# A hybrid decoder layer on one core: where the retention states of the sample tokens are weighted by their queries

## The chip, the cores and the metric

The kernel runs on one core of a Trainium2 chip. Its time is the device time of one execution in microseconds (us): 2566.66 us as the median of three runs (2566.41 to 2567.9). The engines are named as the profile names them: PE (TensorE's matmuls) and PEld (its weight loads), DVE (VectorE), ACT (ScalarE), POOL (GpSimd), and SP (SyncE), whose queue issues the DMAs.

## The reference, cut to what matters

One layer of a decoder is computed for 256 prompt tokens with 16 meta tokens ahead of them, and for 8 sample tokens, one each from eight other requests. The model is 2048 wide. A half-step SwiGLU block, a token mixer and a second half-step SwiGLU block follow one another. The mixer multiplies the input by ten matrices of 2048 x 2048, runs two recurrences on the projections, retention (8 heads of 256 x 256 state) and HGRN2 (16 heads of 128 x 128 state), gates their outputs with sigmoids and multiplies the sum by an output matrix.

For a sample token a retention head does this (one state S of 256 x 256 for each of the 8 requests and each head):

```
S_new = gamma * S + outer(k, v)
o     = q @ S_new          # written here for one token; 256 numbers
```

So a sample's output is its new state, each of its 256 rows multiplied by one number of the query, summed over the rows. The states are outputs too. All inputs and outputs are fp32.

## The kernel before, in words

**Weights.** Every large matrix is read from memory once, in fp32, in *units* of 512 KB: eight blocks of 128 x 128. `load` (L185 to L189) brings a unit into a buffer `raw` by a DMA on SP's queue, ACT rounds it to a first part `whi` (L188), and DVE subtracts to get the rest, `wlo` (L189). Each of the three tiles has three buffers. A DMA for a later unit can start when the `wlo` three units earlier has been computed, and ACT can write a `whi` when PE has finished with the unit three places earlier. PE multiplies each block three times (L218: `xh` by `whi`, `xl` by `whi`, `xh` by `wlo`), so a unit is 24 matmuls of 264 or 280 columns.

**The mixer.** The retention heads and the HGRN2 heads are worked on in eight *steps of heads* u = 0 to 7, one retention head and two HGRN2 heads each. For each u, `project(qkv_groups(u))` computes six pairs of column groups (the pair named `f` first, then `q_h`, `i_h`, and the three of retention), and then `project(gate_groups(u - 1))` computes the gates of the heads before: four groups, in the order g_r with a_r, g_h with a_h, and the two again for the second half. The names of the PSUM tiles begin with `pj_`. One group is 16 inner steps (k = 0 to 15) of two blocks each: four weight units. After every inner step the function `pump` is called. It advances the two generators `mix_hg` and `mix_ret`, which hold everything else of the mixer; `yield n` in one of them lets n inner steps pass. So a `yield` sets between which weight matmuls the small matmuls of the recurrences stand on PE. PE's order is the order in which the program is written. The order on the other engines is set by a scheduler that goes by priorities; the casts of the weights have a higher priority.

**Sample outputs in retention** (end of `mix_ret`). For each u the eight new states lie in four tiles `smr` of 128 x (4 x 256), called `sms[2 * e + c]` in the code: e is the half of the samples, c the half of the 256 rows. They are computed by ACT (L1192) and DVE (L1198) and stored by SP (L1202, `out_srs`). Then 16 fp32 matmuls (L1211) multiply each 128 x 256 piece by a column of the query. The stationary operand is a slice of `qdr`, 128 x 32, zero but for one column; `alone` (L733) has placed the queries so. Four matmuls, for four samples, run in four quarters of PE's columns. The two halves e and c add up in PSUM (`pqr`). The matmuls of HGRN2's samples (L1039, `pq`) stand right ahead of them. After seven more steps the outputs are transposed and added (`po`, `por`), and normalised from there (`pv`, `pvr`); the gate of the g_r group then uses them (`on_r`).

Of the kernel before, what the change touches and what calls it, by code (L numbers as in the profile page):

```python
# [13 lines left out]
AF = mybir.ActivationFunctionType  # L14
ALU = mybir.AluOpType
# [8 lines left out]
NMETA, SEQ, NS = 16, 256, 8  # L24
# [104 lines left out]
def trunk(ctx: ExitStack, tc: tile.TileContext, A, O):  # L129
    nc = tc.nc  # L130
# [108 lines left out]
    def mul(out, a, b):  # L239
        nc.vector.tensor_tensor(out=out, in0=a, in1=b, op=ALU.mult)  # L240

    def bias(b):
        return {} if b is None else {"bias": b}

    def mul_biased(out, o, b, x):
        if b is None:
            mul(out, x, o)
        else:
            nc.vector.scalar_tensor_tensor(out=out, in0=o, scalar=b, in1=x, op0=ALU.add, op1=ALU.mult)

    def add(out, a, b):
        nc.vector.tensor_tensor(out=out, in0=a, in1=b, op=ALU.add)
# [294 lines left out]
    with tc.tile_pool(name="yp", bufs=1) as yp:  # L547
# [7 lines left out]
        with tc.tile_pool(name="mp", bufs=1) as mp:  # L555
# [7 lines left out]
            def tmp(name, shape=(P, T), bufs=1, dt=F32, tag=None):  # L563
                if name in rows:
                    rows[name] = rows[name][1:] + rows[name][:1]
                    return rp.tile(list(shape), dt, tag=rows[name][-1], name=name)
                return mp.tile(list(shape), dt, tag=tag or name, name=name, bufs=bufs)
# [16 lines left out]
            st = {}  # L584
# [5 lines left out]
            qdr = tmp("qdr", (P, 4, ALONE))  # L590
            nc.gpsimd.memset(qdh, 0.0)
            nc.gpsimd.memset(qdr, 0.0)
            qdh_at = [qdh.rearrange("p a c -> p (a c)")[:, 256 * h :] for h in range(2)]
            qdr_at = [qdr.rearrange("p a c -> p (a c)")[:, 2 * ALONE * c :] for c in range(2)]
            vsm = tmp("vsm", (P, P))
            vt2 = tmp("vt2", (P, 2, P))
# [20 lines left out]
            def pump(_=None):  # L617

                for th in list(threads):
                    th[1] -= 1  # L620
                    if th[1] <= 0:
                        th[1] = next(th[0], None)
                        if th[1] is None:
                            threads.remove(th)

            def start(gen, wait):
                threads.append([gen, wait])
# [20 lines left out]
            def evacuate(n, c0, c1, o0, o1, b0, b1):  # L648
                if n == "f":
                    f = tmp("f", (P, 2, T))  # L650
                    k = tmp("k", (P, 2, T))
                    for j, (c, o, b) in enumerate(((c0, o0, b0), (c1, o1, b1))):
                        nc.scalar.activation(f[:, j, :], o, AF.Sigmoid, **bias(b))
                        nc.scalar.activation(f[:, j, :], f[:, j, :], AF.Identity, scale=olb[:, c : c + 1], bias=lb[:, c : c + 1])
                    nc.scalar.activation(k, f, AF.Identity, scale=-1.0, bias=1.0)
                    st["f"], st["k"] = f, k
                elif n == "q_h":
                    q = tmp("q", (P, 2, TL))
                    for j, (o, b) in enumerate(((o0, b0), (o1, b1))):
                        nc.scalar.activation(q[:, j, :], o, AF.Sigmoid, **bias(b))  # L660
                        mul_biased(q[:, j, :], o, b, q[:, j, :])
                    st["q"] = q
                elif n == "i_h":
                    v = st.pop("i_h", None)
                    if v is None:
                        v = tmp("v", (P, 2, T))
                        nc.scalar.copy(v[:, 0, :], o0)
                        nc.scalar.copy(v[:, 1, :], o1)

                    start(mix_hg(c0 // 2, st["f"], st["k"], st["q"], v), {0: 20, 2: 46}.get(c0, 4))  # L670
                elif n in ("q_r", "k_r"):
                    sc, w, x0 = (1.0, TL, NMETA) if n == "q_r" else (KSC, T, 0)
                    r = tmp(n, (P, 2, w))
                    for j, (a, b, op) in enumerate(((cos, sin, ALU.subtract), (sin, cos, ALU.add))):
                        t = tmp("rot", (P, w), bufs=2)
                        for to, o, s, x in ((r[:, j, :], o0, b0, a), (t, o1, b1, b)):
                            nc.vector.scalar_tensor_tensor(
                                out=to, in0=o, scalar=sc if s is None else s, in1=x[:, x0:],
                                op0=ALU.mult if s is None else ALU.add, op1=ALU.mult)
                        nc.vector.tensor_tensor(out=r[:, j, :], in0=r[:, j, :], in1=t, op=op)  # L680
                    st[n] = r
                elif n == "v_r":
                    v = tmp("v", (P, 2, T))
                    nc.scalar.copy(v[:, 0, :], o0)
                    nc.scalar.copy(v[:, 1, :], o1)
                    start(mix_ret(c0 // 2, st["q_r"], st["k_r"], v), 24 if c0 == 2 else 3)
                elif n in ("g_r", "g_h"):
                    sg = tmp("gs", (P, TL), bufs=2)
                    t = tmp("gt", (P, TL), bufs=2)
                    nc.scalar.activation(sg, o0, AF.Sigmoid)  # L690
                    mul(t, sg, o0)
                    sa = tmp("gs", (P, TL), bufs=2)
                    nc.scalar.activation(sa, o1, AF.Sigmoid)
                    mul(t, t, sa)
                    u, e = divmod(c0, 2)
                    while u not in (done_r if n == "g_r" else done_h):
                        pump()
                    if n == "g_r":
                        y = tmp("y", (P, TL))
                        mul(y, t, on_r[u][:, e, :])  # L700
                        st["y"] = y
                    else:
                        y = st["y"]
                        nc.vector.scalar_tensor_tensor(
                            out=t, in0=t, scalar=ngt[:, c0 : c0 + 1], in1=on_h[u][:, e, :], op0=ALU.mult, op1=ALU.mult)

                        ys[c0] = y if c0 < EARLY else yp.tile([P, TL], F32, tag=f"y{c0}", name=f"y{c0}")
                        add(ys[c0], y, t)
                        if c0 < EARLY:
                            split(yh[c0], yl[c0], y)  # L710
# [22 lines left out]
            def alone(qd, q):  # L733
                nc.vector.tensor_copy(
                    qd[:, :, : 128 : 32].rearrange("p (c e) j -> p c e j", e=2),
                    q[:, :, SEQ:].rearrange("p c (e j) -> p c e j", e=2))
# [9 lines left out]
            def mix_hg(u, f, k, q, v):  # L746

                calm = 2
# [14 lines left out]
                sms, vbs = [], []  # L763
# [254 lines left out]
                for h in range(2):  # L1018
# [7 lines left out]
                    for b in range(2):  # L1026
                        nc.vector.scalar_tensor_tensor(
                            out=S[:, b + 1, :], in0=S[:, b, :], scalar=Tt[:, h, b : b + 1],
                            in1=pst[:, (b + 1) * P : (b + 2) * P], op0=ALU.mult, op1=ALU.add)
                    nc.sync.dma_start(O["sgp"][2 * u + h], S[:, 2, :])  # L1030
                if u == 1:
                    yield 2
                    samples(1)
                yield (8, 11, 45)[min(u, 2)]
                pq = mx_bank("pq")
                for h in range(2):
                    for b in range(NS):
                        j = 32 * (b % 4)
                        nc.tensor.matmul(  # L1039
                            pq[j : j + 32, :P], qdh_at[h][:, 32 * b : 32 * b + 32], sms[h][:, b, :],  # L1040
                            start=h == 0 and b < 4, stop=h == 1 and b >= 4, tile_position=(0, j))
# [26 lines left out]
                calm = calm if u else 0  # L1068
# [16 lines left out]
            def mix_ret(u, q, k, v):  # L1085
# [3 lines left out]
                calm = 2  # L1089
                sms = []  # L1090
# [13 lines left out]
                for c in range(2):  # L1104
# [22 lines left out]
                    for x, g, his, i, lo in todo:  # L1127
                        for hi in his:
                            nc.scalar.activation(hi, x, AF.Copy, scale=g)
                        nc.vector.scalar_tensor_tensor(  # L1130
                            out=lo, in0=x, scalar=g, in1=his[i].bitcast(F32), op0=ALU.mult, op1=ALU.subtract)
                    yield 2
                alone(qdr, q)
                vts = [vt[:, 0], vt[:, 1], vs2]
                vrow = rows_out(vt2.rearrange("p c f -> p (c f)")[16:24, :], 256, "vr")

# [25 lines left out]
                for c in range(2):  # L1162
# [9 lines left out]
                    if c == 0:  # L1172
                        gams = [tmp("gam", (P, 1))]
                        nc.gpsimd.tensor_scalar(
                            out=gams[0], in0=so[:, 0:1], scalar1=GAMMA[u], scalar2=GAMMA[u], op0=ALU.min, op1=ALU.max)
# [13 lines left out]
                for e in range(2):  # L1189
# [3 lines left out]
                    for i in (2 * e, 2 * e + 1):  # L1193
                        for c in range(2):
                            for b in (2 * i, 2 * i + 1):
# [3 lines left out]
                                    out=x, in0=vbs[i][:, b - 2 * i, :], scalar=kk, in1=x, op0=ALU.mult, op1=ALU.add)  # L1199
# [1 line left out]
                    for c in range(2):  # L1201
                        nc.sync.dma_start(O["srs"][u, c, :, 4 * e : 4 * e + 4, :], ss[c])  # L1202
                    yield 1 if e else 10 if u == 0 else 6
                yield (11 if u == 0 else 15) + 2 * calm
                pq = mx_bank("pqr")
                scores(pq[:, 256:], 2)
                for e in range(2):
                    for c in range(2):
                        for j in range(4):
                            b = 4 * e + j  # L1210
                            nc.tensor.matmul(  # L1211
                                pq[32 * j : 32 * j + 32, :256], qdr_at[c][:, 32 * b : 32 * b + 32],
                                sms[2 * e + c][:, j, :], start=e + c == 0, stop=e + c == 2, tile_position=(0, 32 * j))
                mul(scr2[:NB2], pq[:NB2, 256 : 256 + NMETA], dt[:NB2, c2:])
                upper_upper_lower(sc2, scr2[:NB2])
                os = tmp("osr", (P, 256))
# [160 lines left out]
```

## Time and profile before

| What | Value |
|---|---|
| median of three runs | 2566.66 us |
| the profiled execution's span | 2563.9 us |
| PE, share of the span and instructions | 2553.4 us, 100%, 23424 |
| DVE | 1702.8 us, 66%, 2827 |
| ACT | 1392.2 us, 54%, 2186 |
| POOL | 57.0 us, 2%, 152 |
| DMA, bytes and mean rate | 536.26 MB, 209 GB/s |

The execution that was profiled spans 2563.9 us between its first and its last instruction; the median of the timed runs is 2.8 us longer, which is what lies around the span. The mixer's steps of heads fill about 825 to 1760 us of the span; the SwiGLU blocks lie ahead of and behind it. A row of the timeline gives start, duration, engine, line, operation and tiles, and, in brackets, the idle time of that engine just before and what ended it. A number with an x behind a row says how many instructions it stands for. PE's matmuls are pipelined: the distance between two starts says more than the duration of one.

### The profile page before, as it was taken

To read this page: it belongs to the slowest core of one execution; us is meant where nothing else is said; L and a number is where in the kernel's file an instruction comes from. 1 tells how busy PE (TensorE), PEld (TensorE's weight loads), DVE (VectorE), ACT (ScalarE), POOL (GpSimd) and SP (SyncE) were. 2 spreads that over 40 slices of the span, in tenths; PEclk is the share of its full clock that TensorE was granted. 3 is DMA by queue.
4 is the path that set the end of the run, shared out by engine and by line. 5 is a ranking of instruction groups with operands and counts; after the bars stand their busy time and mean duration, and the time that the engine had idled before them with its cause. 6 is when DMAs were issued, how large, how long until landed. Compare 5 with 4: busy or idle time off the path is not lost.

```text
span 2563.9 us, 56275 instructions
## 1 busy us (share of the span) xinstructions
PE 2553.4 (100%) x23424; PEld 2534.4 (99%) x23424; DVE 1702.8 (66%) x2827; ACT 1392.2 (54%) x2186; POOL 57.0 (2%) x152
## 2 busy tenths in 40 slices
PE   9999999999999999999999999999999999999999
PEld 9999999999999999999999999999999999999998
DVE  6444544475569878777777777777885555556555
ACT  5444444444456767767676666675564444444443
POOL 0000000000000000000000000000000000000000
PEclk9999999999999999999999999999999999999999
DMA  7555555555555876767676767675556565565554
GB/s 244 183 187 183 187 182 184 186 182 186 184 201 180 287 265 232 264 214 260 212 264 215 259 223 255 224 239 188 196 190 197 194 197 195 194 196 195 195 195 149
DMA packets 156897, 536.26 MB, mean 209 GB/s; under 512 B 17952, under 2 KB 25952, under 8 KB 156640
## 3 DMA queue, kind: packets, MB, share of 16 engines
q1 hardware_dynamic: 156352, 532.37, 62.0%
q8 instruction: 183, 3.00, 0.5%
q14 instruction: 74, 0.61, 0.1%
q10 hardware_dynamic: 288, 0.29, 0.0%
HBM read 501.99 MB, written 30.61 MB: 208 GB/s over the span
## 4 chain that ended last, share of the span: by engine, by line
PE 96%; DVE 2%; ACT 0%; issue 0%; DMA 0%; SPq 0%; ACTq 0%; DVEq 0%
PE up L218 36%; PE dn L218 19%; PE pj_i_h L218 3%; PE pj_g_r L218 3%; PE pj_q_h L218 3%; PE pj_g_h L218 3%; PE pj_a_r L218 3%; PE pj_a_h L218 3%; PE pj_f L218 3%; PE pj_q_r L218 3%; PE pj_k_r L218 3%; PE wo L218 3%; PE pj_v_r L218 3%; DVE wlo L189 1%; PE pqr L1211 1%; PE psr L1168 0%
## 5 line engine op out<-in xcount | busy, mean ns | idle before, releaser
L189 DVE TENSOR_TENSOR wlo<-raw,whi 128x1024 fp32r<-128x1024 f32 (+1 forms) x869 | 1062.2, 1223 | 740.7 <-ACT whi L188 737.3
L188 ACT CAST whi<-raw 128x1024 fp32r<-128x1024 f32 (+1 forms) x870 | 905.7, 1042 | 909.2 <-PE up L218 411.0
L218 PE MATMUL up<-xh,whi 128*128 128x280 f32 (+1 forms) x2624 | 725.6, 280 | 0.6 <-ACT whi L188 0.6
L218 PE MATMUL up<-xh,wlo 128*128 128x280 f32 (+1 forms) x2624 | 725.8, 280 | 0.4 <-DVE wlo L189 0.3
L218 PE MATMUL up<-xl,whi 128*128 128x280 f32 (+1 forms) x2624 | 725.4, 279 | 0.0
L218 PEld LDWEIGHTS up<-xh,wlo 128*128 128x128 f32 x2624 | 492.6, 189 | 1.0 <-DVE wlo L189 1.0
L218 PEld LDWEIGHTS up<-xh,whi 128*128 128x128 f32 x2624 | 492.6, 189 | 0.8 <-ACT whi L188 0.8
L218 PEld LDWEIGHTS up<-xl,whi 128*128 128x128 f32 x2624 | 492.6, 189 | 0.0
L218 PE MATMUL dn<-hh,whi 128*128 128x280 f32 (+1 forms) x1376 | 384.7, 280 | 0.0
L218 PE MATMUL dn<-hh,wlo 128*128 128x280 f32 (+1 forms) x1376 | 384.3, 279 | 0.0
L218 PE MATMUL dn<-hl,whi 128*128 128x280 f32 (+1 forms) x1376 | 384.3, 279 | 0.0
L218 PEld LDWEIGHTS dn<-hh,whi 128*128 128x128 f32 x1376 | 260.1, 189 | 0.1
L218 PEld LDWEIGHTS dn<-hl,whi 128*128 128x128 f32 x1376 | 260.1, 189 | 0.1
L218 PEld LDWEIGHTS dn<-hh,wlo 128*128 128x128 f32 x1376 | 260.1, 189 | 0.0
L218 PE MATMUL pj_k_r<-xh,whi 128*128 128x280 f32 x256 | 74.2, 290 | 0.0
L218 PE MATMUL pj_g_r<-xh,whi 128*128 128x264 f32 x256 | 74.0, 289 | 0.0
L218 PE MATMUL pj_v_r<-xh,whi 128*128 128x280 f32 x256 | 73.8, 288 | 0.0
L218 PE MATMUL pj_v_r<-xh,wlo 128*128 128x280 f32 x256 | 72.4, 283 | 0.3 <-DVE wlo L189 0.3
L218 PE MATMUL pj_g_h<-xh,whi 128*128 128x264 f32 x256 | 72.7, 284 | 0.0
L218 PE MATMUL pj_k_r<-xh,wlo 128*128 128x280 f32 x256 | 72.4, 283 | 0.0
L218 PE MATMUL pj_v_r<-xl,whi 128*128 128x280 f32 x256 | 72.3, 283 | 0.0
L218 PE MATMUL pj_k_r<-xl,whi 128*128 128x280 f32 x256 | 72.3, 283 | 0.0
(421 smaller groups left out, 5263.4 us busy)
## 6 DMA issues: line engine op xcount, KB each, us to landing
raw<-in_w_up SPq DMA_DIRECT2D x343, 512.0 KB, 4.1
raw<-in_w_in SPq DMA_DIRECT2D x320, 512.0 KB, 4.3
raw<-in_w_dn SPq DMA_DIRECT2D x172, 512.0 KB, 3.5
smr<-in_sr SPq DMA_DIRECT2D x32, 512.0 KB, 5.0
out_srs<-smr SPq DMA_DIRECT2D x32, 512.0 KB, 6.7
raw<-in_w_out SPq DMA_DIRECT2D x32, 512.0 KB, 3.9
vbr<-vrd SPq DMA_DIRECT2D x32, 256.0 KB, 4.1
smh<-in_sg SPq DMA_DIRECT2D x16, 512.0 KB, 5.2
```

The lines of the kernel that those rows point to most:

```text
L188: nc.scalar.copy(hi[:, j:jn, :], raw[:, j:jn, :])
L189: nc.vector.tensor_tensor(out=lo[:, j0:j1, :], in0=raw[:, j0:j1, :], in1=hi[:, j0:j1, :].bitcast(F32), op=ALU.subtract)
L218: nc.tensor.matmul(o, w, t, start=start, stop=stop)
L1211: nc.tensor.matmul(pq[32 * j : 32 * j + 32, :256], qdr_at[c][:, 32 * b : 32 * b + 32], sms[2 * e + c][:, j, :], start=e + c == 0, stop=e + ...
```

## The change

For u = 2 to 7 (the *third unit* of heads onward) the two halves c of a sample's state are combined ahead of the matmul. GpSimd (for e = 0, new line L1223) or ScalarE (e = 1, L1221) multiplies the 128 x 256 piece of c = 0 by its queries, one number for each partition, and VectorE (L1224) multiplies the piece of c = 1 by its queries and adds. That is 4 operations on GpSimd, 4 on ScalarE and 8 on VectorE for each u. Then 8 matmuls instead of 16 (L1233) sum over the partitions; their stationary operand `one` is zero but for a column of ones.

The queries are copied by GpSimd to `late_q` (L1215). A copy ahead of it (L1214) reads the newest sigmoid of a gate, `seen`, and so holds GpSimd's work until that tile is there. VectorE's copy in `alone` is left out from u = 2 on. For u = 2 GpSimd also writes zeros and ones once.

The waits in steps change too: 45 becomes 67 in `mix_hg`, and 15 + 4 becomes 25 + 16 in `mix_ret`, with the new operations between the two. So both sets of sample matmuls, and everything behind them in the generators, come 22 inner steps later in PE's order. u = 0 and 1 stay as they are.

```diff
             qdr = tmp("qdr", (P, 4, ALONE))
...
+            one = qdr[:, 0, :64].rearrange("p (e m) -> p e m", e=2)
+            late_q = qdr[:, 1, : 2 * NS].rearrange("p (c b) -> p c b", c=2)
...
                     nc.scalar.activation(sa, o1, AF.Sigmoid)
+                    st["seen"] = sa
                     mul(t, t, sa)
...
-                yield (8, 11, 45)[min(u, 2)]
+                yield (8, 11, 67)[min(u, 2)]
                 pq = mx_bank("pq")
...
-                alone(qdr, q)
+                if u < 2:
+                    alone(qdr, q)
...
-                yield (11 if u == 0 else 15) + 2 * calm
+                yield (11 if u == 0 else 15) + 2 * calm if u < 2 else 25
+                if u == 2:
+                    nc.gpsimd.memset(qdr[:, 0, :64], 0.0)
+                    for e in range(2):
+                        nc.gpsimd.memset(one[:, e, e : e + 1], 1.0)
+                if u > 1:
+                    nc.gpsimd.tensor_copy(late_q[:, 0, :1], st["seen"][:, :1])
+                    nc.gpsimd.tensor_copy(late_q, q[:, :, SEQ:])
+                    for e in range(2):
+                        s0, s1 = sms[2 * e : 2 * e + 2]
+                        for b in range(4):
+                            g = [late_q[:, c, 4 * e + b : 4 * e + b + 1] for c in range(2)]
+                            if e:
+                                nc.scalar.activation(s0[:, b, :], s0[:, b, :], AF.Copy, scale=g[0])
+                            else:
+                                nc.gpsimd.tensor_scalar(out=s0[:, b, :], in0=s0[:, b, :], scalar1=g[0], scalar2=None, op0=ALU.mult)
+                            nc.vector.scalar_tensor_tensor(
+                                out=s0[:, b, :], in0=s1[:, b, :], scalar=g[1], in1=s0[:, b, :], op0=ALU.mult, op1=ALU.add)
+                    yield 16
                 pq = mx_bank("pqr")
                 scores(pq[:, 256:], 2)
                 for e in range(2):
-                    for c in range(2):
+                    for c in range(2 if u < 2 else 1):
                         for j in range(4):
                             b = 4 * e + j
                             nc.tensor.matmul(
-                                pq[32 * j : 32 * j + 32, :256], qdr_at[c][:, 32 * b : 32 * b + 32],
-                                sms[2 * e + c][:, j, :], start=e + c == 0, stop=e + c == 2, tile_position=(0, 32 * j))
+                                pq[32 * j : 32 * j + 32, :256], qdr_at[c][:, 32 * b : 32 * b + 32] if u < 2 else one[:, e, :],
+                                sms[2 * e + c][:, j, :], start=e + c == 0, stop=e + c == 2 if u < 2 else e == 1, tile_position=(0, 32 * j))
```

The order of the engines' instructions before and after is shown for u = 3, on three engines. PE first, at the sample matmuls. Before, they stand inside a g_r/a_r group, after its inner step 10:

```order
L218 MATMUL pj_a_r_15214<-xh_10_9275,wlo_15277 128x264
L1039 MATMUL pq<-smh,qdh 32x128 x16
L1141 MATMUL pqr<-q_r,k_r 16x16 x2
L1211 MATMUL pqr<-smr,qdr 32x256 x16
L218 MATMUL pj_g_r_15213<-xh_11_9279,whi_15276 128x264
```

After the change they stand behind the first inner step of the next u's `f` group, 22 steps later, and the last set has half as many:

```order
L218 MATMUL pj_f_15506<-xh_0_9235,wlo_15509 128x280
L1042 MATMUL pq<-smh,qdh 32x128 x16
L1145 MATMUL pqr<-q_r,k_r 16x16 x2
L1233 MATMUL pqr<-smr,qdr 32x256 x8
L218 MATMUL pj_f_15505<-xh_1_9239,whi_15508 128x280
```

So two weight groups less one step run on PE without the sample matmuls between their steps, and the first step of `f` now has them behind it.

On DVE the place is the stretch from g_r's inner step 8 to the next `f` group. The names `gt` and `y` are gate products, `scr`, `sc`, `cen` and `osr` follow the sample matmuls. Before:

```order
L189 TENSOR_TENSOR wlo_15396<-raw_15394,whi_15395 128x8x128
L240 TENSOR_TENSOR scr_8637<-pqr,dtab 16x16
L255 TENSOR_TENSOR sc_8642<-scr_8637,sc_8642 16x16
L1081 TENSOR_REDUCE cen<-osr 128x1
L1082 TENSOR_SCALAR cen<-cen 128x1
L1083 TENSOR_TENSOR osr<-osr,cen 128x256
L189 TENSOR_TENSOR wlo_15465<-raw_15463,whi_15464 128x8x128
L240 TENSOR_TENSOR gt<-gs,pj_g_r_15213 128x264
L189 TENSOR_TENSOR wlo_15495<-raw_15493,whi_15494 128x8x128
L240 TENSOR_TENSOR gt<-gt,gs 128x264
L742 COPY on_h<-po 128x2x8
```

After:

```order
L189 TENSOR_TENSOR wlo_15407<-raw_15405,whi_15406 128x8x128
L240 TENSOR_TENSOR gt<-gs,pj_g_r_15224 128x264
L189 TENSOR_TENSOR wlo_15437<-raw_15435,whi_15436 128x8x128
L240 TENSOR_TENSOR gt<-gt,gs 128x264
L1224 SCALAR_TENSOR_TENSOR smr<-smr,qdr 128x256
L240 TENSOR_TENSOR y<-gt,on_r 128x264
L1224 SCALAR_TENSOR_TENSOR smr<-smr,qdr 128x256 x3
L189 TENSOR_TENSOR wlo_15467<-raw_15465,whi_15466 128x8x128
L1224 SCALAR_TENSOR_TENSOR smr<-smr,qdr 128x256 x4
L189 TENSOR_TENSOR wlo_15509<-raw_15507,whi_15508 128x8x128
```

The small operations behind the sample matmuls have left this stretch; four of the new operations stand between two casts of weights, and four more between the next two.

On ACT, in the same stretch after the change (`gs` are the sigmoids of the gates; the fourth row makes the tile that `seen` names):

```order
L188 CAST whi_15406<-raw_15405 128x8x128
L692 ACTIVATE gs<-pj_g_r_15224 128x264
L188 CAST whi_15436<-raw_15435 128x8x128
L695 ACTIVATE gs<-pj_a_r_15225 128x264
L1221 ACTIVATE smr<-smr,qdr 128x256 x4
L188 CAST whi_15466<-raw_15465 128x8x128
```

ACT's four multiplications stand between two casts. GpSimd's whole order there, after the change, is this:

```order
L1192 COPY sro<-k_r 128x8
L1214 COPY qdr<-gs 128x1
L1215 COPY qdr<-q_r 128x16
L1223 TENSOR_SCALAR smr<-smr,qdr 128x256 x4
L913 COPY meta<-K 128x2x16
```

Before the change, the second, third and fourth of these rows are not there.

## The prediction

> **What bounds the kernel now.** I read the page's busy times first, then the chain of waits, then single stretches of the timeline.
>
> ```profile
> PE 2553.4 (100%) x23424; PEld 2534.4 (99%) x23424; DVE 1702.8 (66%) x2827; ACT 1392.2 (54%) x2186; POOL 57.0 (2%) x152
> PE 96%; DVE 2%; ACT 0%; issue 0%; DMA 0%; SPq 0%; ACTq 0%; DVEq 0%
> ```
>
> PE is busy all the time and 96% of the chain is its own work. So the only certain gain is matmul time taken away, and any new wait of PE is added to the time. The matmuls at issue, for u = 3:
>
> ```profile
> 1190.44 0.28 PE L218 MATMUL pj_a_r<-xh,wlo 128*128 128x264 f32 x1
> 1190.65 1.08 PE L1039 MATMUL pq<-smh,qdh 128*32 128x128 f32 x32
> 1191.65 1.89 PE L1211 MATMUL pqr<-smr,qdr 128*32 128x256 f32 x29
> 1193.47 0.38 PE L218 MATMUL pj_g_r<-xh,whi 128*128 128x264 f32 x1
> ```
>
> The weight matmuls before and after the sample matmuls start 3.03 us apart (1193.47 - 1190.44); their usual pitch is 10.80 / 96 = 0.1125 us by the next rows, which each count one whole group of columns by 96 matmuls:
>
> ```profile
> 1097.31 10.80 PE pj_q_h L218 x96
> 1108.11 11.44 PE pj_i_h L218 x96
> ```
>
> A weight unit is 24 matmuls: 2.70 us (264 columns) or 2.86 us (280 columns). PE never stalls there, but by how little?
>
> ```profile
> 1188.64 0.19 PEld L218 LDWEIGHTS pj_g_r<-xh,wlo 128*128 128x128 f32 x1
> 1202.49 0.19 PEld L218 LDWEIGHTS pj_g_h<-xh,wlo 128*128 128x128 f32 x1
> 1187.26 1.22 DVE L189 TENSOR_TENSOR wlo<-raw,whi 128x1024 fp32r<-128x1024 f32 x1
> 1196.02 1.23 DVE L189 TENSOR_TENSOR wlo<-raw,whi 128x1024 fp32r<-128x1024 f32 x1 [0.21 <-ACT whi L188]
> 1198.47 1.23 DVE L189 TENSOR_TENSOR wlo<-raw,whi 128x1024 fp32r<-128x1024 f32 x1 [0.81 <-ACT whi L188]
> ```
>
> The first row is PE's first use of `wlo` of the unit that holds inner steps 8 to 11 of g_r; call that unit A. Its `wlo` was ready at 1187.26 + 1.22 = 1188.48, 0.16 us before. Three units later (A+3, second row) the `wlo` of 1196.02 was ready 5.24 us early. What made that slack is not a faster supply. It is PE's pauses: from 1188.64 to 1202.49 are 13.85 us for three units of 2.70 us, so 5.75 us went to small matmuls (`pq`, `pqr`, `po`, `por`). The supply itself is at its limit, as the windows show (us, then busy time of PE, PEld, DVE, ACT, POOL, the granted clock, the DMA share, GB/s):
>
> ```profile
> 1168.00:1188.00 20.00, 20.00 (x181) 20.00 (x180) 16.95 (x33) 13.52 (x20) 1.40 (x3) 1.00 0.82 275
> 1188.00:1202.00 14.00, 14.00 (x165) 12.85 (x164) 9.97 (x22) 7.48 (x15) 0.00 (x0) 1.00 0.96 332
> 1211.00:1224.00 13.00, 13.00 (x112) 13.00 (x111) 11.10 (x21) 10.74 (x16) 0.00 (x0) 1.00 0.50 157
> 1194.94 1.05 ACT L188 CAST whi<-raw 128x1024 fp32r<-128x1024 f32 x1 [0.23 <-DMA raw<-in_w_in]
> 1197.39 1.04 ACT L188 CAST whi<-raw 128x1024 fp32r<-128x1024 f32 x1 [0.19 <-DMA raw<-in_w_in]
> 1191.35 0.33 SPq L185 DMA_DIRECT2D raw<-in_w_in  x1
> ```
>
> The DMA engines are 0.96 busy from 1188 to 1202, and the casts of A+3 and A+4 (1194.94, 1197.39) end waits for DMAs; the `raw` of the latter was issued at 1191.35, 6 us earlier. So the supply has no reserve just where the change takes PE's pauses out.
>
> **The change part by part. What it removes:** 8 of 16 matmuls for each u, which run four at a time, so 8 rounds become 4. A round takes (1.89 - 0.38) / 7 = 0.216 us (0.38 is one matmul, next row), so 0.86 us for each u and 6 x 0.86 = 5.2 us in all. That is 0.2% of the time and the most that can be won.
>
> ```profile
> L1211 PE MATMUL pqr<-smr,qdr x256: 379/379/403, 859.8 to 1698.6; 128*32 128x256 f32 x128
> ```
>
> **What it moves.** The sample matmuls and what follows them leave A to A+5 and stand 22 steps later. PE then wants the weights early: counted from 1188.64, A+3 at +8.10 (1196.74), A+5 at +13.50 (1202.14), A+6, the first unit of `f`, at +16.20. Against the ends of `wlo` above: A+3 was ready at 1197.25, so **0.5 us of stall**. A+4's cast ended 1199.70 (1198.47 + 1.23) and was needed at 1199.44 + 0.5, so it holds. Neither comes earlier by the change, since both hang on DMAs issued before anything that has moved. The DVE work that leaves (`scr` to `osr`) was behind those waits, too.
>
> **What it adds** comes behind A+4's cast, ahead of A+5's on both engines. Prices:
>
> ```profile
> 1182.61 2.06 DVE L1198 SCALAR_TENSOR_TENSOR smr<-vbr,sro,smr 128x256 f32<-128x256 f32 x5
> 1199.61 0.43 DVE L240 TENSOR_TENSOR gt<-gt,gs 128x264 f32<-128x264 f32 x1
> 1198.35 0.38 ACT L693 ACTIVATE gs<-pj_a_r 128x264 f32<-128x264 f32 x1
> L998 ACT ACTIVATE smh<-smh,meta 128x128 f32<-128x128 f32 x128 | 41.1, 391 | 0.4
> L1192 ACT ACTIVATE smr<-smr,gam 128x1024 f32<-128x1024 f32 x16 | 17.6, 1142 | 9.2 <-POOL gam L1174 9.2
> 1148.36 0.23 POOL L1103 COPY tails<-k_r 128x48 f32<-128x48 f32 x1 [4.01 <-DVE k_r L680]
> 1172.35 0.19 POOL L1188 COPY sro<-k_r 128x8 f32<-128x8 f32 x1
> 1170.10 1.21 DVE L189 TENSOR_TENSOR wlo<-raw,whi 128x1024 fp32r<-128x1024 f32 x1
> 1170.18 1.17 POOL L1174 TENSOR_SCALAR gam<-sro 128x1 f32<-128x1 f32 x1 [9.92 <-ACT sro L1170]
> ```
>
> - DVE, multiply and add: 2.06 / 5 = 0.41 us each, eight for each u (3.3 us).
> - ACT, 128 x 256: between 0.38 (264 columns) and 391 + 128 x (1142 - 391) / 896 = 498 ns. I take 0.44.
> - GpSimd, 128 x 256: no row has it. From 8 and 48 columns follow 0.001 us a column, so 0.23 + 208 x 0.001 = 0.44; I take 0.42 and keep 0.6 as the upper end. The dearest row is `gam`, 1.17 us for a single column, but it ends with the `wlo` that runs beside it (1171.35 and 1171.31), so I read it as 0.2 us behind a wait. It also tells that GpSimd doesn't proceed beside a DVE operation of two SBUF tiles. The new operations on DVE are of that kind, so I take the two engines as taking turns.
>
> The Trainium skill says so outright ("SBUF — State Buffer", "Who interferes with whom"): GpSimd and an operation of VectorE with two inputs in SBUF hold a shared port exclusively, and the later one blocks. The `gam` row agrees (1.17 against 0.19 us). That the new operation on VectorE takes the port is shown by no run here; by that rule the sum is the one below, without it the lower bound.
>
> For u = 3: `seen` is ready at 1198.73 (1198.35 + 0.38), GpSimd gets through after A+4's `wlo` at 1199.70, two short copies of 0.2 us and their hand-overs make 1200.2. Four turns of 0.42 + 0.41 and `y` (0.43, like `gt`) between them end at 1203.95, A+5's `wlo` at 1205.2. ACT meanwhile goes 1200.2 + 4 x 0.44 + 1.05 = 1203.0, so it isn't last. PE needs A+5 at 1202.14 + 0.5 = 1202.64: **2.5 us of stall**. Then four more additions and a cast on DVE, 1205.2 + 1.65 + 1.23 = 1208.1, against 1202.64 + 2.5 + 2.70 = 1207.84: **0.3 us**. In `f` the sample matmuls give PE its pause back, about 2.2 us, and the stall ends. Sum for u = 3: 3.3 us.
>
> The other five u have a better start. u = 4, by the same three places:
>
> ```profile
> 1314.98 0.19 PEld L218 LDWEIGHTS pj_g_r<-xh,wlo 128*128 128x128 f32 x1
> 1320.88 1.05 ACT L188 CAST whi<-raw 128x1024 fp32r<-128x1024 f32 x1
> 1324.50 1.23 DVE L189 TENSOR_TENSOR wlo<-raw,whi 128x1024 fp32r<-128x1024 f32 x1 [0.50 <-ACT whi L188]
> ```
>
> A+4's `wlo` ends 10.75 us after A's use (11.06 in u = 3), and the cast of A+3 stood behind ACT's copies of the sample outputs, which move away, so perhaps 10.5. The chain of 5.5 us from there (1199.70 to 1205.2) ends at 16.0 against 13.5 plus 0.1: 2.4, and 0.1 to 0.3 around it; I take 2.5. **Sum: 3.3 + 5 x 2.5 = 15.8 us of new stalls, less 5.2 us of matmuls: +10.6 us.** The span goes from 2563.9 to 2574.5, and with the 2.76 us by which the median of 2566.66 lies above the span, to **2577 us**.
>
> **At no cost:** GpSimd's writes of ones (u = 2, once), two copies and the missing `alone` are off PE's path; without their 0.5 us the chain would begin at 1199.7, so they are in it. The next u's two loads of states, which SP issued behind `pqr`, now wait for the additions and stand behind two weight loads on the queue; nobody needs them before the next u, and they delay no weight before A+5. In `f` the cover is thin (DVE 11.10 and ACT 10.74 of 13 us, third window), but PE's own pauses move there with the work. At u = 7 no `f` follows, and the gate forces `pvr` two steps early; I bound that at two steps, 1.35 us, once, and take 0.
>
> **Bounds.** Low: GpSimd works beside DVE. Then u = 3 ends A+5's `wlo` by ACT's path, 1203.0 + 1.23 = 1204.25, 1.6 us of stall and 2.4 in all; the others, from 10.5, 1.35 each: 9.2 - 5.2 = +4.0, 2570.7 us. High: 0.6 for a GpSimd operation, four turns longer by 0.7 us, six times: +4.3, 2581.5 us; and a chain that starts 0.25 later each (no gain from ACT's copies) 2583.
>
> **The rivals.**
>
> *A: no stall, 2561.5 us (not slower).* The loads leave the queue's worst stretch, each `raw` lands sooner, and the chain fits. It needs A+5's `wlo` 2.5 us earlier. The next row gives the wait from issue to landing; the two loads of states, 1 MB, make about 3 us of the queue at 332 GB/s.
>
> ```profile
> raw<-in_w_in SPq DMA_DIRECT2D x8, 512.0 KB, 5.8
> ```
>
> It decides where `raw` comes in 4.3 us and both engines work side by side (1.5 + 1.0 us). Against it: the `raw` of A+4 was issued at 1191.35, ahead of those loads, which follow `pqr`. Gain 5.2 us.
>
> *B: a mild stall, 2567 to 2571.8 us.* The lower bound above, or part of the DMA gain of A: some 0.9 to 1.7 us a u.
>
> *C: GpSimd's operations cost what the one long row says,* 1.17 us each, with DVE's hidden beneath. u = 3: 1200.2 + 4 x 1.17 + 0.41 + 1.23 = 1206.5, so 3.9 instead of 2.5; six times 1.3 to 1.4 more: +8, 2585 us. Against it: the row has a wait in it. For it: no row of this size exists.
>
> *D: the change doesn't reach PE,* because PE now waits for the additions at `pqr`. They are done by 1207 (four behind A+5's cast), `pqr` stands at about 1209; 0 to 1 us each. It would raise the forecast by up to 5, inside C's range.
>
> **How the numbers follow.** The likeliest case, stalls of 2 to 3 us a u, 2571.8 to 2583 us: 0.48. C and D above 2583: 0.20. B: 0.22. A: 0.10. A measurement of this kernel tells 0.2% from no change, 5.1 us. So: faster (below 2561.5) only in the better half of A and a little beyond, 0.08, since the whole gain is just 0.2%; the same (2561.5 to 2571.8) in B and the rest of A, 0.21; slower 0.71. Predicted 2577 us, range 2564 to 2586 us; the likeliest case alone has 2571.8 to 2583.
>
> **What would show it.** `pqr` with 8 matmuls in about 1.05 us; idle time of PE before weight loads of A+3 and A+5, put down to `wlo` (DVE), some 2 to 3 us for each u; four turns of GpSimd and DVE of 0.83 us between two casts. Wrong if the additions overlap GpSimd's multiplications and end by 1202.7, if `raw` of A+4 lands more than a microsecond earlier, or if PE stalls in the `f` group instead.

## The result and the profile after

| | before | after |
|---|---|---|
| median | 2566.6 us | 2587.91 us (2585.29 to 2589.8) |
| ratio | | 1.0082, 95% interval 1.0068 to 1.0097 |
| span of the profiled execution | 2563.9 us | 2584.9 us |

The change makes the kernel 21 us slower. The forecast said slower by 10.6 us with a range up to 2586: the sign is right, the size is half of what came, and the range misses by 2 us.

The page after, its busy times, the chain of waits and one group of PE's:

```profile
PE 2559.5 (99%) x23328; PEld 2540.0 (98%) x23328; DVE 1723.2 (67%) x2869; ACT 1397.2 (54%) x2208; POOL 87.5 (3%) x191
PE 87%; DVE 4%; DMA 4%; ACT 2%; issue 1%; POOL 1%; SPq 0%; ACTq 0%; DVEq 0%; POOLq 0%
L218 PE MATMUL pj_g_h<-xh,wlo 128*128 128x264 f32 x256 | 73.9, 289 | 13.8 <-DVE wlo L189 13.8
```

Two things stand out. The last row, in the list of the costliest groups, has 13.8 us in which PE stood idle ahead of a matmul that needs `wlo`; before, this group had none. Of the 13.8 us, 13.3 are six waits of 2.04 to 2.28 us, one for each u. And PE's busy time rose by 6.1 us although it has 96 matmul records fewer and each matmul does what it did. So the matmuls themselves became slower somewhere. The windows show where, here around unit A+5 of u = 4 (us, busy time of PE, PEld, DVE, ACT and POOL, the granted clock, the DMA share, GB/s):

```profile
1330.00:1336.60 6.60, 6.60 (x61) 6.60 (x60) 4.30 (x8) 4.46 (x8) 4.32 (x6) 1.00 0.74 253
1336.60:1338.90 2.30, 0.28 (x3) 0.09 (x1) 2.09 (x4) 1.50 (x2) 0.62 (x1) 1.00 0.11 25
1338.90:1342.60 3.70, 3.67 (x17) 3.67 (x18) 3.70 (x6) 0.00 (x0) 0.00 (x0) 0.54 0.85 279
```

PE does nothing for most of the 2.3 us of the second row. In the 3.7 us after it PE is busy at a granted clock of 0.54, and gets 17 matmuls done instead of some 33 at the usual 0.1125 us: half of 3.7 us is lost once more. The timeline of PE (start, duration, engine, line, operation) has the edge:

```profile
1336.61 0.28 PE L218 MATMUL pj_g_h<-xl,whi 128*128 128x264 f32 x1
1338.93 0.39 PE L218 MATMUL pj_g_h<-xh,wlo 128*128 128x264 f32 x1 [2.04 <-DVE wlo L189]
1339.55 0.43 PE L218 MATMUL pj_a_h<-xh,wlo 128*128 128x264 f32 x1
1339.77 0.43 PE L218 MATMUL pj_g_h<-xh,whi 128*128 128x264 f32 x1
...
1342.61 0.28 PE L218 MATMUL pj_g_h<-xl,whi 128*128 128x264 f32 x1
1342.72 0.28 PE L218 MATMUL pj_g_h<-xh,wlo 128*128 128x264 f32 x1
```

The pitch is 0.22 us from 1339.55 on and 0.11 us again from 1342.61. The same picture stands at the same place, the last unit of the g_h group, for u = 2 to 6: two matmul starts lie 2.3 to 2.6 us apart (2.04 to 2.28 us of idle time in the brackets), and 12 to 17 slow matmuls follow. For u = 7 PE idles as long, but stays at full rate:

```profile
1726.92 0.28 PE L218 MATMUL pj_g_h<-xl,whi 128*128 128x264 f32 x1
1729.47 0.38 PE L218 MATMUL pj_g_h<-xh,wlo 128*128 128x264 f32 x1 [2.27 <-DVE wlo L189]
1729.69 0.28 PE L218 MATMUL pj_a_h<-xh,whi 128*128 128x264 f32 x1
1729.80 0.28 PE L218 MATMUL pj_a_h<-xl,whi 128*128 128x264 f32 x1
```

What made the cast late? GpSimd and VectorE ahead of the cast of u = 4:

```profile
1331.81 1.23 DVE L189 TENSOR_TENSOR wlo<-raw,whi 128x1024 fp32r<-128x1024 f32 x1 [0.98 <-ACT whi L188]
1332.12 0.96 POOL L1214 COPY qdr<-gs 128x1 f32<-128x1 f32 x1 [25.02 <-ACT gs L695]
1333.14 0.29 POOL L1215 COPY qdr<-q_r 128x16 f32<-128x16 f32 x1
1333.53 3.69 POOL L1223 TENSOR_SCALAR smr<-smr,qdr 128x256 f32<-128x256 f32 x4
1334.49 0.69 DVE L1224 SCALAR_TENSOR_TENSOR smr<-smr,qdr 128x256 f32<-128x256 f32 x1 [1.11 <-POOL smr L1223]
1335.11 0.42 DVE L240 TENSOR_TENSOR y<-gt,on_r 128x264 f32<-128x264 f32 x1
1335.45 0.69 DVE L1224 SCALAR_TENSOR_TENSOR smr<-smr,qdr 128x256 f32<-128x256 f32 x1
1336.35 0.70 DVE L1224 SCALAR_TENSOR_TENSOR smr<-smr,qdr 128x256 f32<-128x256 f32 x1 [0.21 <-POOL smr L1223]
1337.25 0.48 DVE L1224 SCALAR_TENSOR_TENSOR smr<-smr,qdr 128x256 f32<-128x256 f32 x1 [0.21 <-POOL smr L1223]
1337.65 1.22 DVE L189 TENSOR_TENSOR wlo<-raw,whi 128x1024 fp32r<-128x1024 f32 x1
1335.08 1.98 ACT L188 CAST whi<-raw 128x1024 fp32r<-128x1024 f32 x2
```

One multiplication on GpSimd takes 3.69 / 4 = 0.92 us. VectorE's first, third and fourth addition wait for it (ahead of the second stands `y`), and its cast starts at 1337.65. ScalarE had the first part of that unit ready at about 1336.1, so the cast could have started 1.5 us earlier.

### The profile page after: what moved, and what is told of

Read it like the earlier page. It is cut to its first block, busy times and chain, and to the rows that moved or that the text cites. A ratio compares the mean times of both kernels' runs of the same rounds, so it can differ in the third digit from the quotient of the medians.

```text
span 2584.9 us, 56199 instructions
## 1 busy us (share of the span) xinstructions
PE 2559.5 (99%) x23328; PEld 2540.0 (98%) x23328; DVE 1723.2 (67%) x2869; ACT 1397.2 (54%) x2208; POOL 87.5 (3%) x191
## 4 chain that ended last, share of the span: by engine, by line
PE 87%; DVE 4%; DMA 4%; ACT 2%; issue 1%; POOL 1%; SPq 0%; ACTq 0%; DVEq 0%; POOLq 0%
PE up L218 37%; PE dn L218 18%; PE pj_q_h L218 3%; PE pj_i_h L218 3%; PE pj_k_r L218 3%; PE wo L218 3%; PE pj_q_r L218 3%; DMA raw<-in_w_in 3%; PE pj_f L218 3%; PE pj_v_r L218 3%; DVE wlo L189 2%; PE pj_g_r L218 2%; PE pj_a_r L218 2%; PE pj_g_h L218 1%; PE pj_a_h L218 1%
## 5 line engine op out<-in xcount | busy, mean ns | idle before, releaser
L218 PE MATMUL pj_g_h<-xh,wlo 128*128 128x264 f32 x256 | 73.9, 289 | 13.8 <-DVE wlo L189 13.8
L218 PE MATMUL pj_a_h<-xh,whi 128*128 128x264 f32 x256 | 72.6, 284 | 0.0
L218 PE MATMUL pj_a_h<-xl,whi 128*128 128x264 f32 x256 | 72.5, 283 | 0.0
```

The costliest lines, as they stand in the source:

```text
L218: nc.tensor.matmul(o, w, t, start=start, stop=stop)
```

## The experiments

Beside the kernel before, each run has its own runs of the kernel before on the same chip (medians 2566.9 to 2567.2 us). The theory: late casts, made by the added operations' place and GpSimd's duration, plus the clock's fall behind each long idle time. The rival: the move itself, which takes PE's pauses from a stretch in which the weights only just come in time.

**The move alone.** The kernel before, with the two waits of the change:

```diff
-                yield (8, 11, 45)[min(u, 2)]
+                yield (8, 11, 67)[min(u, 2)]
-                yield (11 if u == 0 else 15) + 2 * calm
+                yield (11 if u == 0 else 15) + 2 * calm if u < 2 else 41
```

> The move alone: all queries 22 steps later from u = 2 on, with the 16 matmuls of before and nothing on GpSimd, ScalarE or VectorE added. Theory (the added operations stand ahead of the cast and make the stall of 2.2 to 2.4 us for each u, and the half rate behind it another 1.7 to 1.9 us): no stall of PE over 0.9 us, no matmuls at half rate, 2565 to 2569 us. Rival (taking PE's pauses out of a stretch in which the DMA engines are 0.96 busy is enough by itself): stalls of 1 to 2.5 us for each u stay, 2575 to 2588 us.

Measured: 2568.46 us, ratio 1.0009 (0.9999 to 1.0018). PE's waits for `wlo` in g_h come to 2.8 us in all, no one over 0.77 us, and no matmul runs at half rate. The move by itself costs 1.3 us by the medians (the interval goes from 0.3 us less to 4.6 us more); it uses up the slack, and leaves little.

**The gain alone.** The kernel before, with the eight matmuls of c = 1 left out from u = 2 on and nothing in their place (the samples' outputs then lack half of the rows):

```diff
-                    for c in range(2):
+                    for c in range(2 if u < 2 else 1):
                         for j in range(4):
```

> The kernel before with the 8 matmuls of c = 1 simply left out for u = 2 to 6 and 7 (the samples' outputs lack half of the rows), nothing added and nothing moved: the gain by itself. Theory (four rounds of 0.216 us less for each u): 5.2 us less, 2561 to 2562.5 us. Rival (PE's pause there is slack for weights that come late, so that a shorter pause is given back as a stall): 2564 to 2567 us.

Measured: 2562.39 us, ratio 0.9983 (0.9975 to 0.9992). That is 4.5 us less, against 5.2 forecast. The rival has a small part in it: in the profiled execution PE has two new waits for weights in g_r, 1.01 us at u = 3 and 0.37 us at u = 5. So the gain that the change could have had is about 5 us.

**Without GpSimd's multiplications.**

```diff
                             if e:
                                 nc.scalar.activation(s0[:, b, :], s0[:, b, :], AF.Copy, scale=g[0])
-                            else:
-                                nc.gpsimd.tensor_scalar(out=s0[:, b, :], in0=s0[:, b, :], scalar1=g[0], scalar2=None, op0=ALU.mult)
```

> The change without GpSimd's four multiplications for each u (the samples of e = 0 then lack a factor); the copies on GpSimd, ScalarE's multiplications and all eight additions stay. Theory (GpSimd's 4 x 0.92 us set the pace of the additions ahead of the cast): the four additions and y take 4 x 0.41 + 0.43 = 2.1 us instead of 4.3, the cast of the last g_h unit then waits for ScalarE's, the stall falls from 2.3 to about 0.6 us and nothing runs at half rate: 2565 to 2569 us. Rival (the eight additions on VectorE and ScalarE's multiplications are what is late): stall over 1.5 us with the half rate, 2578 to 2588 us.

Measured: 2571.48 us, ratio 1.0017 (1.0007 to 1.0026). This is 16 us less than the change and nothing runs at half rate, but it misses its expectation by 2.5 us. PE still waits 6.9 us for `wlo` in g_h, in nine pieces of 0.77 us, in u = 2, 3 and 7 two of them for each u.

**All multiplications on ScalarE,** in the same place, a kernel that computes everything:

```diff
-                            if e:
-                                nc.scalar.activation(s0[:, b, :], s0[:, b, :], AF.Copy, scale=g[0])
-                            else:
-                                nc.gpsimd.tensor_scalar(out=s0[:, b, :], in0=s0[:, b, :], scalar1=g[0], scalar2=None, op0=ALU.mult)
+                            nc.scalar.activation(s0[:, b, :], s0[:, b, :], AF.Copy, scale=g[0])
```

> The change with all eight multiplications on ScalarE, none on GpSimd (its two copies stay); places and steps as in the change. Theory (GpSimd's 0.92 us for each multiplication is what made the additions slow; ScalarE takes 0.43): as in the kernel without GpSimd's multiplications, stalls of 0.5 to 1 us instead of 2.3, no half rate: 2568 to 2573 us. Rival (any eight operations in this place make the cast as late): 2580 to 2590 us.

Measured: 2569.81 us, ratio 1.0012 (1.0003 to 1.0021): 18 us of the 21 are gone by the choice of the engine alone. VectorE's chain for the same cast of u = 4 in this kernel:

```profile
1326.98 0.43 DVE L240 TENSOR_TENSOR gt<-gt,gs 128x264 f32<-128x264 f32 x1
1328.04 0.48 DVE L1221 SCALAR_TENSOR_TENSOR smr<-smr,qdr 128x256 f32<-128x256 f32 x1 [0.63 <-ACT smr L1220]
1328.44 0.43 DVE L240 TENSOR_TENSOR y<-gt,on_r 128x264 f32<-128x264 f32 x1
1328.79 1.27 DVE L1221 SCALAR_TENSOR_TENSOR smr<-smr,qdr 128x256 f32<-128x256 f32 x3
1330.17 1.22 DVE L189 TENSOR_TENSOR wlo<-raw,whi 128x1024 fp32r<-128x1024 f32 x1
```

From the end of `gt` to the start of the cast are 1330.17 - 1327.41 = 2.8 us here, and 1337.65 - 1333.38 = 4.3 us with GpSimd. The 1.5 us between them take PE's idle time at this place from 2.0 to 0.7 us, and no matmul runs at half rate.

**The idle time filled.** The change, with ten fp32 matmuls of no use (PE's list shows them as `dm`) in the place in which PE idled; and the same with five:

```diff
-                    yield 16
+                    yield 11
+                    dm = mx_bank("dm")
+                    for i in range(10):
+                        nc.tensor.matmul(dm[:, :P], ident, ident, start=True, stop=True)
+                    yield 5
```

> The change with ten extra fp32 matmuls of 128 columns on PE (into a bank that nobody reads) behind step 11 of each g_h group in which PE stalls, so that PE works, to no use, for about 2.2 us while the cast is late. Theory (the clock falls because PE idled): the stall is filled, the matmuls behind it run at full rate, and the time falls by what the half rate cost, 9 us, to 2577 to 2581 us. Rival (the half rate has another cause, or the extra matmuls only add): 2586 to 2600 us.

> The change with five instead of ten extra matmuls in the late cast's place: about half of the idle time is filled, 1.1 to 1.4 us stay idle. If the fall of the clock needs an idle time of near 2 us (stalls of 0.9 to 1.9 us had none so far, those of 2.2 to 2.4 us had), nothing runs at half rate and the time is that of ten: 2578 to 2582 us. If any idle time of a microsecond costs the clock: 2585 us or more.

Measured: 2580.3 us (ratio 1.005, 1.0035 to 1.0065) with ten, 2579.54 us (1.0051, 1.0037 to 1.0064) with five. Both are about 8 us faster than the change, although PE does more. The third of the windows above, in the kernel with ten, where the clock is 1.00:

```profile
1338.90:1342.60 3.70, 3.70 (x68) 2.97 (x67) 2.39 (x4) 1.50 (x3) 0.00 (x0) 1.00 0.98 318
```

The edge of the idle time of u = 4 in the kernel with five:

```profile
1336.83 0.28 PE L218 MATMUL pj_g_h<-xl,whi 128*128 128x264 f32 x1
1338.40 0.38 PE L218 MATMUL pj_g_h<-xh,wlo 128*128 128x264 f32 x1 [1.30 <-DVE wlo L189]
1338.62 0.28 PE L218 MATMUL pj_a_h<-xh,whi 128*128 128x264 f32 x1
1338.73 0.28 PE L218 MATMUL pj_a_h<-xl,whi 128*128 128x264 f32 x1
```

With an idle time of 1.3 us instead of 2.0 the clock holds, and the pitch is 0.11 us at once. With five the sum of PE's waits for `wlo` in g_h is 9.6 us, with ten 2.8 us (1.8 and 0.3 us of them ahead of the first of the six places): the 5.4 between the rest are filled with work of no use, so the two times are alike. The difference to the change is the clock's share.

**HGRN2's queries put back.** The change, with 45 instead of 67 steps in `mix_hg`, so that two of PE's pauses return:

```diff
-                yield (8, 11, 67)[min(u, 2)]
+                yield (8, 11, 45)[min(u, 2)]
```

> The change with one number put back: HGRN2's queries at 45 steps as before, retention's in the change's place, GpSimd's multiplications as in the change. VectorE's order then has six additions ahead of the late cast instead of four. Theory (lateness of the cast against the need): the need comes 2.0 us later by pq's and po's pauses, the cast 0.8 us later by two additions: stall of 2.3 + 0.8 - 2.0 = 1.1 us, no half rate: 2566 to 2571 us. Rival (PE's pauses have no part in it): 2585 us or more.

Measured: 2602.59 us, ratio 1.0142 (1.0128 to 1.0156). The theory missed it; the time lies where the rival had put it, but it comes from another wait. PE no longer waits for `wlo` in the gates at all; it waits for HGRN2's norm:

```profile
1209.96 1.28 DVE L1224 SCALAR_TENSOR_TENSOR smr<-smr,qdr 128x256 f32<-128x256 f32 x3 [0.21 <-POOL smr L1223]
1211.16 1.22 DVE L189 TENSOR_TENSOR wlo<-raw,whi 128x1024 fp32r<-128x1024 f32 x1
1212.29 0.87 DVE L1224 SCALAR_TENSOR_TENSOR smr<-smr,qdr 128x256 f32<-128x256 f32 x2
1213.08 0.17 DVE L745 COPY on_h<-po 128x16 f32<-128x16 f32 x1
...
1214.31 0.59 PE L237 MATMUL pv<-hhi,ones_r 128*128 128x264 f32 x1 [3.10 <-ACT hhi L225]
```

VectorE's copy `on_h`, with which that norm begins, stands behind all eight additions, and `pv` is 3.1 us late, at half rate too (0.59 us for a matmul of 264 columns). So in the change the later place of HGRN2's queries also takes their norm out of the additions' way.

**Retention's part later,** behind the first step of f with HGRN2's queries at 45, once with GpSimd as in the change and once with ScalarE:

```diff
-                yield (8, 11, 67)[min(u, 2)]
+                yield (8, 11, 45)[min(u, 2)]
-                yield (11 if u == 0 else 15) + 2 * calm if u < 2 else 25
+                yield (11 if u == 0 else 15) + 2 * calm if u < 2 else 41 if u < 7 else 25
```

> The change with its operations in another place: HGRN2's queries back at 45 steps (where they were before), and for u = 2 to 6 the multiplications and additions 16 steps later (behind the first step of f), their 8 matmuls another 16 steps behind them; u = 7 keeps the change's 25 and 16. Theory (the place is what cost): the weights are 2 to 5 us ahead there, no stall over 0.5 us, and the 5.2 us of matmul time are won: 2560 to 2564 us. Rival (eight additions on VectorE and the turns with GpSimd make the casts late wherever they stand): 2568 us or more.

> The kernel with HGRN2's queries at 45 steps and retention's operations behind the first step of f, which took 2589 us with GpSimd's multiplications (1.23 us each there), now with all eight on ScalarE. Theory (GpSimd's multiplications are what was slow, in f too): the stall of 1.0 us at q_h goes, por's wait of 1.6 us shrinks below 0.8 us: 2564 to 2573 us. Rival (it is the place, whichever engine multiplies): 2582 us or more.

Measured: 2589.23 us (1.0082, 1.0065 to 1.0099) with GpSimd, 2590.21 us (1.0092, 1.0078 to 1.0106) with ScalarE. The times are the rivals' both times: here the place costs, whichever engine multiplies. (The 1.23 us of the second expectation is a mean; most of GpSimd's multiplications took 0.93 us, and one 2.1 us.) With GpSimd PE also waits 0.9 us for weights at q_h in each of these u, which the first theory had excluded; with ScalarE that wait is gone. But the main wait moved to `por`, as the list of waits around u = 3 with ScalarE says (engine, line, waited for, us in total, times, longest):

```profile
PE por L744 <- DVE osr L1086: 2.7, 1, 2.7
```

VectorE's timeline in the same kernel shows why:

```profile
1232.87 1.07 DVE L240 TENSOR_TENSOR T<-T 128x68 f32<-128x68 f32 x5
1233.89 1.23 DVE L189 TENSOR_TENSOR wlo<-raw,whi 128x1024 fp32r<-128x1024 f32 x1
1235.03 0.41 DVE L1084 TENSOR_REDUCE cen<-osr 128x1 f32<-128x256 f32 x1
1235.36 0.43 DVE L240 TENSOR_TENSOR K<-K,f 128x272 f32<-128x272 f32 x1
1236.19 0.42 DVE L1086 TENSOR_TENSOR osr<-osr,cen 128x256 f32<-128x256 f32 x1
```

The sample outputs `osr` are centred behind the next head's decay products `T`, and PE needs them for `por`. This wait, 1.5 to 2.5 us for each of the five u with GpSimd, is 2.7 us with ScalarE, and the granted clock falls behind four of those five.

**Three attempts at a faster version,** all with ScalarE's multiplications and HGRN2's queries at 45 steps: with the additions two steps apart; with retention's part 12 steps later and held back until HGRN2's first norm is done; and that with u = 7 alone at 67.

```diff
                                 out=s0[:, b, :], in0=s1[:, b, :], scalar=g[1], in1=s0[:, b, :], op0=ALU.mult, op1=ALU.add)
+                            yield 2
-                    yield 16
```

> As the one with all multiplications on ScalarE, and besides HGRN2's queries back at 45 steps, so that two of PE's pauses (pq 1.1 us, po 0.9 us) return to the stretch ahead of the late cast; the additions are two inner steps apart in the program, of which VectorE's order keeps a little (one, one, three, then three). Theory (the stall is the lateness of one cast against PE's need, which a pause moves): the cast at about 1337.9 in the time of the change's profile against a need of 1338.8, no stall over 0.4 us, the saved matmuls show: 2561 to 2564.5 us. Rival (the saving is eaten by casts elsewhere): 2566 us or more.

```diff
                 mul(on[:, h, :], on[:, h, :], r)
+                st["normed"] = on
-                yield (11 if u == 0 else 15) + 2 * calm if u < 2 else 25
+                yield (11 if u == 0 else 15) + 2 * calm if u < 2 else 37 if u < 7 else 25
-                    nc.gpsimd.tensor_copy(late_q[:, 0, :1], st["seen"][:, :1])
+                    nc.gpsimd.tensor_copy(late_q[:, 0, :1], st["normed"][:, 0, :1] if u < 7 else st["seen"][:, :1])
```

> An attempt at a faster version: all eight multiplications on ScalarE, HGRN2's queries back at 45 steps, and for u = 2 to 6 the retention operations 12 steps later and held back (by GpSimd's first copy) until the first HGRN2 norm of this u is done, their 8 matmuls 16 steps behind them; u = 7 as in the change but on ScalarE. Theory (nothing is late for PE there: HGRN2's norm is ahead of the additions, weights are 2 to 5 us ahead in f, ScalarE takes 0.43 us): no stall of PE over 0.5 us, 2561 to 2565 us. Rival (eight additions and their casts are too much for f also, or por then waits for the sample outputs): 2567 us or more.

```diff
-                yield (8, 11, 45)[min(u, 2)]
+                yield (8, 11, 45)[min(u, 2)] if u < 7 else 67
```

> The attempt at a faster version, with u = 7 alone having HGRN2's queries at 67 steps as in the change (with 45 the last gate group waited 4.3 us for HGRN2's norm, and more behind it). Theory (that wait goes, the others stay as they were): 2574.2 less 5 to 7, 2566 to 2569.5 us. Rival (the last u is late in either way): 2572 us or more.

Measured: 2569.44 us (1.0011, 1.0002 to 1.002), 2574.2 us (1.0022, 1.0012 to 1.0032), 2568.37 us (1.0008, 0.9999 to 1.0017). None beats the kernel before. In the first two the theory missed and the rival's range held. In the first, PE loses 0.5 to 1.1 us at `pv` in u = 3 to 6 (1.66 to 2.24 us between the weight matmuls around it, against 1.15 before). In the second, u = 7 alone lost 4.3 us at the same `pv`: 2.6 us of idle time, and 6.8 us at a granted clock of 0.50 behind it. The third gives that back, as expected. No place was found in which eight multiplications and eight additions are free, and the gain of about 5 us did not pay for any that was tried.

## Why the prediction was wrong

**The gain** was right: four rounds for each u, 5.2 us forecast, 4.5 us measured by itself. In the `f` group, where the sample matmuls stand after the change, PE needs 0.86 us less for each u than in the move alone, as forecast.

**The stall at A+5** was right in place and size: 2.4 to 2.5 us forecast for each u, 2.2 to 2.4 us found (the distance of the two starts less the usual pitch), and it waits for the cast that stands behind GpSimd's multiplications and VectorE's additions. The six add up to 14.3 us; the forecast's stalls added up to 15.8. The half microsecond at A+3 and the 0.3 at A+6 were not there in u = 3 and 4.

**The step that failed is the sum's last one:** it took a stall as its own length. Behind each stall of u = 2 to 6 the granted clock was 0.50 for 3.41 us. With each idle time cut to 1.75 us or less (five extra matmuls) the clock held and the time fell by 8.4 us, with ten by 7.6: that is the missing term. PE's starts in the profiled execution give the same: behind the six stalls the matmuls need 8.6 us more than at their usual pitch. So 14.3 us of stalls and 8.6 us of slow matmuls, less 5.2 us for the matmuls saved, make 17.7 of the 21.0 us by which the two spans differ. The 3.3 us that are left are spread over short delays and were not isolated; 1.6 us of them stand ahead of the first stall, and it is not shown that the change made them.

The Trainium skill states this rule ("TensorE: Matmul & The Clock Gate", "What's actually happening"): the clock is halved after an idle window of about 3.4 us that runs freely, and comes back after as long a busy one. The recovery agrees with the trace (3.41 us at 0.50). The idle time that sufficed here is shorter than that page's window (2.04 us in the row above).

Why u = 7 kept its clock after 2.27 us, the trace shows. In the kernel after, the clock falls at 1079.76, 1209.46, 1339.17, 1468.88 and 1598.58: 129.70 to 129.71 us apart, which is 38 times 3.413 us. Another 38 steps on is 1728.29, in the middle of the idle time of u = 7 (1727.20 to 1729.47). Here are two such steps around the stall of u = 4 and two around that of u = 7:

```profile
1335.76:1339.17 3.41, 1.36 (x12) 1.17 (x12) 2.99 (x5) 2.34 (x3) 1.46 (x2) 1.00 0.17 47
1339.17:1342.58 3.41, 3.41 (x17) 3.41 (x17) 3.41 (x6) 0.00 (x0) 0.00 (x0) 0.50 0.87 291
1724.88:1728.29 3.41, 2.11 (x17) 1.72 (x15) 2.84 (x6) 2.72 (x5) 2.88 (x4) 1.00 0.41 151
1728.29:1731.70 3.41, 2.23 (x19) 2.23 (x20) 3.41 (x6) 1.04 (x1) 0.00 (x0) 1.00 0.34 95
```

For u = 4 all 2.04 us lie in one step, in which PE is busy for 1.36 us, and the clock falls at its end. For u = 7 they are split into 1.09 and 1.18 us (the first step holds another short wait of 0.20), and it does not fall. Steps of 3.41 us, counted from each kernel's own falls, fit the other profiled kernels too: a step with 2.03 us or more of idle time was always followed by a fall, one with 1.77 us or less never; of four steps between 1.84 and 1.92 us, two were. An idle time of 2.33 us in the third attempt at a faster version, split into 1.90 and 0.43, had none.

The forecast had not weighed this rule: every window that it shows of the profile before has a clock of 1.00, and PE's longest idle time there is 1.05 us, so the price of a first idle time could not be read from it.

**GpSimd's price** was wrong, and its error was hidden. Forecast: 0.42 us, taking turns with VectorE's 0.41. Measured: 0.92 us, with VectorE's additions beside it:

```profile
L1223 POOL TENSOR_SCALAR smr<-smr,qdr x24: 917/926/986, 1074.8 to 1726.8; 128x256 f32<-128x256 f32 x24
L1224 DVE SCALAR_TENSOR_TENSOR smr<-smr,qdr x48: 476/481/696, 1075.8 to 1730.5; 128x256 f32<-128x256 f32 x48
```

Four times 0.92 is 3.7 us, and the turns of 0.83 with `y` between them made 3.75 us. That the size of the stall came out was luck, the sum being right for the wrong reason: of the mechanism, rival C (long operations on GpSimd, VectorE's hidden beneath) was nearer. The two engines do not take turns here, as the forecast had taken from the `gam` row: the second, third and fourth multiplication run on while VectorE adds. But the additions that run beside GpSimd take 0.69 us instead of 0.48, so VectorE does pay something. With the casts of the weights it is another matter: the copy of one column at 1332.12 took 0.96 us and ended with the cast that ran beside it (1333.08 and 1333.04), as the `gam` row before had shown.

**Of the rivals,** A needed raw weights that land earlier, and B either that or a GpSimd that works beside VectorE. GpSimd did, but at 0.92 us for each multiplication this made no shorter chain. ScalarE's multiplications in the same place came out in B's range, 2569.81 us. (B and the rest of A add up to 0.24 for the same time, not to 0.21, which leaves 0.68 for slower.) D did not happen: no wait of PE for the additions at `pqr` is in the trace.

## What to carry to other kernels

Where PE is the bound, price a stall by its length and by what the clock does after it: here a stall of 2.2 to 2.5 us cost 1.5 to 1.8 us more where about 2 us of it fell into one 3.41 us step of the clock, and an idle time of 1.75 us or less its length alone, so shortening a stall by a microsecond can be worth two. An operation that replaces PE's work has to be priced on the engine that gets it, at its size, before anything else, and the place has to be checked against every wait behind it: moved once the wait was for weights, moved again for a norm, and a third time for the outputs. The small certain gain (here 0.2%) did not pay for that in any place that was tried.

## What the runs showed of the hardware that was not expected

- The granted clock fell to 0.50 for 3.41 us behind idle times of 2.04 to 2.28 us, in five of six cases in one execution; idle times of 0.26 to 1.75 us (the kernel with five extra matmuls) had none in six of six.
- What decides is the idle time within one of the clock's steps of 3.41 us: 2.27 us split over two steps did nothing.
- One GpSimd multiplication of 128 x 256 fp32 by a number for each partition takes 0.92 us, against 0.43 us on ScalarE (1.71 us for four).
- VectorE's addition of two SBUF tiles runs beside it, at 0.69 us instead of 0.48.
